# Expert weights in rows of 8 KB, and one pool of 8 KB places in place of pairs of 4 KB tiles

## The chip, the core and the metric

One core of one Trainium2 chip runs the whole program. The metric is the device time of one execution in microseconds. Before the change three runs took 1977.47, 1981.33 and 1982.41 us; their median is 1981.33 us.

## What is computed

Three blocks of a model run one after the other on 256 tokens of width 1024 in fp32. Only the end of the third block is touched here, the expert layer:

```python
def expert_choice_ffn(h, w_router, w_gate, w_up, w_down):
    b, s, d = h.shape
    cap = EC_CAPACITY * s // N_EXPERTS
    affinity = jax.nn.softmax((h @ w_router).astype(jnp.float32), axis=-1)
    top_val, top_idx = lax.top_k(affinity.transpose(0, 2, 1), cap)
    xe = jax.vmap(lambda hb, ib: hb[ib])(h, top_idx)
    act = jax.nn.silu(jnp.einsum('becd,edf->becf', xe, w_gate)) * jnp.einsum('becd,edf->becf', xe, w_up)
    ye = jnp.einsum('becf,efd->becd', act, w_down) * top_val[..., None].astype(h.dtype)
    return jax.vmap(lambda yb, ib: jnp.zeros((s, d), yb.dtype).at[ib.reshape(-1)].add(yb.reshape(-1, d)))(ye, top_idx)
```

There are 16 experts; each takes 32 of the tokens. An expert has a gate and an up matrix of 1024 x 2048 and a down matrix of 2048 x 1024, that is 8 MB each (here and below 1 MB of weights is 1024 KB, one load; GB/s count bytes in powers of ten). All 48 matrices, 384 MB, are read once from the chip's memory. After the experts comes the last norm.

## The kernel before, in words

`block3` ends with a product in split precision (`gemm_fm` with `tail=True`, called in `last`): `load_w` (L282) brings a chunk of weights into pool `ring`, and `split_w` (L287) splits it into a high and a low part, tiles `wh` and `wl` of pool `hl`. Its result, with the residual added (L1758), is the tile `x3a` of pool `res`. `experts` reads `x3a` for the router's logits (L1798), for the squares of the norm (L1790) and for the transposes that bring tokens into rows (L1824). Then follow the routing on VectorE, the one-hot matrices, and the gathers `pxe` (L1866) that build `xe`, the tokens of each expert.

The weights of the experts come through one function, `load` (L1876), always on SyncE's DMA queue, in program order. It goes round 21 places, each for 1 MB: 13 in the pools `er0` to `er3` on the right side of the memory, which open as earlier stages end, 3 in `ring`, 3 in `hl` and 2 in `res`. A place is free again when the matmuls on its last content are done. Places of `hl` are pairs of tiles of 128 x 1024, so that a load there is two DMAs of 512 KB (L1890, or L1892 in the last expert); all others are one tile of 128 x 2 x 1024 and one DMA (L1885), but for the last expert's down matrix, where there are two everywhere (L1892).

What one row of a DMA is differs. A piece of a gate or up matrix (`up`, L1902 its matmuls) is 128 rows of the matrix, and a row has 2048 numbers: 8 KB in one run, cut into two runs of 4 KB where the place is a pair. A piece of a down matrix is 256 rows of 1024 numbers, two runs of 4 KB in each partition (matmuls L1974). The last expert's down matrix is cut by columns, 512, 256 and 256 wide, so that the end of the kernel can begin on the first columns (matmuls L1996); its runs are 2 KB and then 1 KB.

The first expert's gate and up products (`pgu0`) use loads 1 to 16 and are made inside `experts`, between the gathers. `run` does the rest: loads 17 to 21, the first of the down matrix, go to `hl` and `res`, and load 22 takes the first place of `er0` again, when the first matmuls of `pgu0` are done. `body` opens the pool `ew` for `run` after block 3's pool has closed, and closes `hl` and `res` (`K.late`) after `run`.

Of the kernel before, what the change touches and what calls it, by code (L numbers as in the profile page):

```python
# [10 lines left out]
F32 = mybir.dt.float32  # L11
# [5 lines left out]

S = 256
D = 1024
BIG = 1e30  # L20
EPS = 1e-6

# [141 lines left out]
def layout(x):  # L164
    x = {k: np.asarray(v) for k, v in x.items()}
    a = {}
    ca, coff = const_pack()
    a.update(ca)
    parts = vec_parts(x)
    voff, _ = offsets(parts)  # L170
    a["vecs"] = np.ascontiguousarray(np.concatenate([np.asarray(v, np.float32) for v in parts.values()], 1))
    xt = lambda t: np.ascontiguousarray(t.T.reshape(8, 128, S).transpose(1, 0, 2))
    a["x"] = xt(x["x"][0])
    a["mem"] = xt(x["mem_3"][0])
    a["w_ada"] = np.ascontiguousarray(x["w_ada"][0].T.reshape(12, 2, 128, D).transpose(0, 2, 1, 3)).reshape(12, 128, 2 * D)
    a["crow"] = x["c"]
    w = x["w_in"][0]
    a["w_in"] = wchunks(np.concatenate([w[:, :2048], w[:, 2056:]], 1), 256)
    a["w_ba"] = np.ascontiguousarray(w[:, 2048:2056].reshape(8, 128, 8).transpose(1, 0, 2))
    rows = lambda *names: wchunks(np.concatenate([x[k][0] for k in names], 0), 256)  # L180
    a["w_mg1"] = rows("w_proj_dn", "w_proj_mb")
    a["w_out"] = wchunks(x["w_out"][0], 256)
    w = x["w_in_2"][0]
    a["w_in2"] = wchunks(np.concatenate([w[:, :1536], w[:, 1544:]], 1), 256)
    a["w_if"] = np.ascontiguousarray(w[:, 1536:1544].reshape(8, 128, 8).transpose(1, 0, 2))
    a["lru_w"] = np.ascontiguousarray(np.stack([
        x["lru_wa_2"][0].reshape(2, 128, 64), x["lru_wx_2"][0].reshape(2, 128, 64)], 0).transpose(2, 0, 1, 3))
    a["w_mg2"] = rows("w_out_lru_2", "w_out_mlstm_2", "w_out_sb_2")
    a["w_o2"] = wchunks(x["w_o_2"][0], 256)
    w = x["w_ffn_in_2"][0]  # L190
    a["w_f1"] = np.ascontiguousarray(np.concatenate(
        [w[:, :2816].reshape(1024, 22, 1, 128), w[:, 2816:].reshape(1024, 22, 1, 128)], 2).reshape(1024, 5632))
    a["w_f1"] = wchunks(a["w_f1"], 256)
    w = x["w_ffn_out_2"][0]
    a["w_f2a"] = wchunks(w[:1024], 256)
    a["w_f2b"] = wchunks(w[1024:2048], 256)
    a["w_f2c"] = wchunks(w[2048:], 256)
    a["w_in3"] = wchunks(x["w_in_3"][0], 256)
    pad = np.zeros((6, 7, 127), x["na_rpb_3"].dtype)
    pad[:, :, 48:79] = x["na_rpb_3"][0, :, 4:11]  # L200
    a["rpb"] = np.stack([pad[:, :, 63 - c:127 - c] for c in range(64)], 0)
    a["lora"] = np.ascontiguousarray(np.concatenate([x["rw_w2_3"][0], x["rw_a2_3"][0]], 1).transpose(1, 0, 2))
    a["g2"] = x["rw_g2_3"][0]
    a["w_mkv"] = wchunks(x["w_mem_kv_3"][0], 256)
    a["w_mg3a"] = rows("w_branch_na_3", "w_branch_mem_3")
    a["w_mg3b"] = rows("w_branch_rw_3")
    a["w_out3"] = wchunks(x["w_out_3"][0], 256)
    a["w_rt"] = np.zeros((128, 8, 32), x["w_router_3"].dtype)
    a["w_rt"][:, :, :16] = x["w_router_3"][0].reshape(8, 128, 16).transpose(1, 0, 2)
    a["w_eg"] = x["w_exp_gate_3"][0]  # L210
    a["w_eu"] = x["w_exp_up_3"][0]
    a["w_ed"] = x["w_exp_down_3"][0]
    a["g_fin"] = x["norm_final_g_3"].reshape(1, 1024)
    return {k: np.ascontiguousarray(v) for k, v in a.items()}, coff, voff

# [3 lines left out]
ES = [3, 3, 5, 2]  # L219
RB = 3  # L220
PB = [3, 3, 2]
HP = None
HB = 3


class Core:
# [1543 lines left out]
def experts(K, last, ep, tmp, pool, out):  # L1770

    nc, A, V, C, tc = K.nc, K.A, K.V, K.C, K.tc
# [43 lines left out]
    for t in range(2):  # L1816
        i = nc.scalar.activation(aff[:, t], zl[:, t], AF.Exp, scale=rs[:, t:t + 1], accum_out=su[:, t:t + 1])
# [52 lines left out]
        else:  # L1870
            nc.vector.tensor_scalar(d, p, V("g_ffn3", k), None, op0=ALU.mult)

    slots = [p for p, n in zip(K.er, ES) for _ in range(n)] + [K.ring] * RB + [K.hl] * HB + [K.res] * 2
    cnt = [0]

    def load(src, g=None):  # L1876

        pool = slots[cnt[0] % len(slots)]
        cnt[0] += 1
        if pool is K.hl:  # L1880
            w = [pool.tile([128, 1024], F32, tag=t, name="w" + t) for t in ("wh", "wl")]
        else:
            w = pool.tile([128, 2, 1024], F32, tag="x" if pool is K.res else "w", name="w")
            if g is None:
                nc.sync.dma_start(w, src.rearrange("i p n -> p i n"))  # L1885
                return w[:, 0], w[:, 1]
            w = w[:, 0], w[:, 1]
        for i in range(2):
            if g is None:
                nc.sync.dma_start(w[i], src[i])  # L1890
            else:
                nc.sync.dma_start(w[i].rearrange("p (g n) -> p g n", g=g), src[i].rearrange("g p n -> p g n"))  # L1892
        return w

    def up(src, e, before=None):
        pg = K.psum([128, 512], "pgu", "g")
        for k in range(8):
            if before is not None:
                before(k)
            w = load(src[e, k * 128:k * 128 + 128, :].rearrange("p (i n) -> i p n", i=2))  # L1900
            for j in range(4):
                nc.tensor.matmul(pg[32 * j:32 * j + 32], xe[:, k, e * 32:e * 32 + 32],  # L1902
                                 w[j // 2][:, j % 2 * 512:j % 2 * 512 + 512], start=k == 0, stop=k == 7)
        return pg
# [6 lines left out]
    def run(work):  # L1911
# [1 line left out]
        gr = work.tile([1, 1024], F32, name="gr")  # L1913
        sm = work.tile([128, 2, 3], F32, name="fsm")
        rs = work.tile([128, 2], F32, name="frs")
        parts = [(0, 512), (512, 768), (768, 1024)]

        def add(pvt, ye, c0, c1):

# [26 lines left out]
        for e in range(16):  # L1946
# [20 lines left out]
            pd = [K.psum([128, 512], f"pd{i}") for i in range(2)]  # L1967
            if e < 15:
                for c in range(8):
                    w = load(A["w_ed"][e, c * 256:c * 256 + 256, :].rearrange("(i p) n -> i p n", p=128))  # L1970
                    for i in range(2):
                        j, q = divmod(2 * c + i, 4)
                        for hh in range(2):
                            nc.tensor.matmul(pd[hh][32 * q:32 * q + 32], at[:, q, 32 * j:32 * j + 32],  # L1974
                                             w[i][:, hh * 512:hh * 512 + 512], start=j == 0, stop=j == 3)
                nc.scalar.copy(ye[:, 0:512], pd[0])  # L1976
                nc.vector.tensor_copy(ye[:, 512:1024], pd[1])  # L1977
                for c0 in (0, 512):
                    for _ in add(pvt, ye, c0, c0 + 512):
                        pass  # L1980
                continue
# [6 lines left out]
            for n, (c0, c1) in enumerate(parts):  # L1988
                m = c1 - c0
                g = 1024 // m  # L1990
                p = pd[c0 // 512][:, c0 % 512:c0 % 512 + m]
                for i in range(0, 16, 2 * g):
                    w = load(A["w_ed"][e, i * 128:(i + 2 * g) * 128, c0:c1].rearrange("(i g p) n -> i g p n", i=2, g=g), g)
                    for u in range(2 * g):
                        j, q = divmod(i + u, 4)
                        nc.tensor.matmul(p[32 * q:32 * q + 32], at[:, q, 32 * j:32 * j + 32],  # L1996
                                         w[u // g][:, u % g * m:u % g * m + m], start=j == 0, stop=j == 3)
                h = c0 + m // 2
                nc.scalar.copy(ye[:, c0:h], p[:, 0:m // 2])
                nc.vector.tensor_copy(ye[:, h:c1], p[:, m // 2:])  # L2000
                for t, a in add(pvt, ye, c0, c1):
                    finish(t, n, a)
# [6 lines left out]
@with_exitstack  # L2009
def body(ctx: ExitStack, tc: tile.TileContext, A, out, coff, voff):  # L2010
    nc = tc.nc
    K = Core(ctx, tc, A, coff, voff)
    K.load_vecs()
    K.load_consts("g", K.const)
    xt = K.res.tile([128, 8, S], F32, tag="x", name="x0")
    nc.sync.dma_start(xt, A["x"])
    mem = Memory(K)
    norms = TwoNorms(K)
    with tc.tile_pool(name="b1", bufs=1) as pool:
        xt = block1(K, xt, pool)  # L2020
    K.groups.pop("b1")
    with tc.tile_pool(name="b2", bufs=1) as pool:
        xt = block2(K, xt, pool, mem, norms)
    K.groups.pop("b2")
    with tc.tile_pool(name="b3", bufs=1) as pool:
        last = block3(K, xt, pool, mem, norms)
        ep = ctx.enter_context(tc.tile_pool(name="ep", bufs=1, side="right"))
        with tc.tile_pool(name="et", bufs=1) as tmp:
            run = experts(K, last, ep, tmp, pool, out)
    with tc.tile_pool(name="ew", bufs=1) as work:  # L2030
        run(work)
    K.late.close()

# [14 lines left out]
```

## Time and profile before

| | us |
|---|---|
| median of the runs | 1981.33 |
| the profiled execution's own time | 1979.57 |
| its span from first to last instruction | 1977.6 |
| TensorE busy | 1649.7 (83%) |
| VectorE busy | 771.7 (39%) |
| ScalarE busy | 590.2 (30%) |
| 16 DMA engines, mean rate over the span | 282 GB/s |

Busy times are those of one profiled execution. A TensorE matmul's end is modelled, so its busy share says little of how near to its peak it is. The mean rate hides two halves: up to about 1040 us the DMA engines are idle much of the time, and from there to the end they move the experts' weights.

### The profile page before, as it was taken

To read this page: it belongs to the slowest core of one execution; us is meant where nothing else is said; L and a number is where in the kernel's file an instruction comes from. 1 tells how busy PE (TensorE), PEld (TensorE's weight loads), DVE (VectorE), ACT (ScalarE), POOL (GpSimd) and SP (SyncE) were. 2 spreads that over 40 slices of the span, in tenths; PEclk is the share of its full clock that TensorE was granted. 3 is DMA by queue.
4 is the path that set the end of the run, shared out by engine and by line. 5 is a ranking of instruction groups with operands and counts; after the bars stand their busy time and mean duration, and the time that the engine had idled before them with its cause. 6 is when DMAs were issued, how large, how long until landed. Compare 5 with 4: busy or idle time off the path is not lost.

```text
span 1977.6 us, 28659 instructions
## 1 busy us (share of the span) xinstructions
PE 1649.7 (83%) x11882; PEld 1062.5 (54%) x11882; DVE 771.7 (39%) x1529; ACT 590.2 (30%) x1159; POOL 106.8 (5%) x123
## 2 busy tenths in 40 slices
PE   3999989999999999989979776677777677767776
PEld 2998989899999998868974111111111111111111
DVE  7797767657655676855571000000000000000001
ACT  3655555764554454633441000000000000000001
POOL 0000000000000121300020000000000000000000
PEclk9998989999999999979999888888878889777888
DMA  7442643344545553322689999999999999999998
GB/s 298 171 149 89 230 170 117 138 141 173 177 174 186 179 198 128 108 76 88 235 310 375 414 415 415 415 417 416 416 416 415 416 416 414 414 415 417 418 416 293
DMA packets 106917, 557.04 MB, mean 282 GB/s; under 512 B 10530, under 2 KB 17058, under 8 KB 61859
## 3 DMA queue, kind: packets, MB, share of 16 engines
q1 hardware_dynamic: 106786, 555.21, 72.1%
q8 instruction: 93, 1.52, 0.3%
q14 instruction: 38, 0.30, 0.0%
HBM read 554.12 MB, written 1.05 MB: 281 GB/s over the span
## 4 chain that ended last, share of the span: by engine, by line
PE 46%; DMA 41%; DVE 8%; ACT 2%; issue 1%; SPq 1%; POOL 1%; DVEq 0%; ACTq 0%
DMA w<-in_w_eg 15%; DMA w<-in_w_eu 13%; PE psg L313 10%; PE psg L311 10%; PE psg L312 10%; DMA w<-in_w_ed 5%; DMA wwl<-in_w_eu 4%; DVE wl L302 2%; PE pgu L1902 2%; PE pd L1974 2%; DMA wwh<-in_w_eu 1%; DVE w L664 1%; DMA wwl<-in_w_eg 1%; DMA wwh<-in_w_eg 1%; PE psg L328 1%
## 5 line engine op out<-in xcount | busy, mean ns | idle before, releaser
L1902 PE MATMUL pgu<-w,xe 128*32 128x512 f32 x1768 | 304.2, 782 | 155.1 <-DMA w<-in_w_eu 89.1
L302 DVE TENSOR_TENSOR wl<-w,wh 128x512 fp32r<-128x512 f32 (+1 forms) x510 | 330.6, 690 | 183.2 <-ACT wh L300 170.6
L300 ACT CAST wh<-w 128x512 fp32r<-128x512 f32 x516 | 287.7, 607 | 253.1 <-PE psg L312 223.3
L1902 PEld LDWEIGHTS pgu<-w,xe 128*32 128x32 f32 x1768 | 42.9, 121 | 393.6 <-DMA w<-in_w_eu 222.3
L1974 PE MATMUL pd<-w,at 128*32 128x512 f32 x808 | 186.0, 637 | 48.5 <-DMA w<-in_w_ed 43.0
L1952 DVE TENSOR_TENSOR gg<-gg,pgu 128x512 f32<-128x512 f32 x16 | 11.0, 688 | 503.9 <-PE pgu L1902 500.3
L1974 PEld LDWEIGHTS pd<-w,at 128*32 128x32 f32 x808 | 42.2, 115 | 183.5 <-DMA w<-in_w_ed 112.7
L1977 DVE COPY ye<-pd 128x512 f32<-128x512 f32 x15 | 10.4, 692 | 294.5 <-PE pd L1974 294.5
L313 PE MATMUL psg<-n3hh,wl 128*128 128x256 f32 x344 | 103.0, 299 | 3.2 <-POOL wl L302 1.7
L311 PE MATMUL psg<-h1h,wh 128*128 128x256 f32 x352 | 103.0, 293 | 0.0
L311 PE MATMUL psg<-n3hh,wh 128*128 128x256 f32 x344 | 101.5, 295 | 1.6 <-ACT wh L300 1.6
L313 PE MATMUL psg<-h1h,wl 128*128 128x256 f32 x352 | 102.2, 290 | 0.0
L312 PE MATMUL psg<-h1l,wh 128*128 128x256 f32 x352 | 101.7, 289 | 0.0
L1957 ACT COPY at<-pat 128x512 f32<-128x512 f32 x16 | 9.4, 585 | 308.6 <-PE pat L1955 297.1
L312 PE MATMUL psg<-n3hl,wh 128*128 128x256 f32 x344 | 100.8, 293 | 0.1
L312 PE MATMUL psg<-n2fhl,wh 128*128 128x256 f32 x352 | 100.0, 284 | 0.2
L313 PE MATMUL psg<-n2fhh,wl 128*128 128x256 f32 x352 | 99.8, 283 | 0.0
L311 PE MATMUL psg<-n2fhh,wh 128*128 128x256 f32 x352 | 99.6, 283 | 0.0
L1951 ACT ACTIVATE gg<-pgu 128x512 f32<-128x512 f32 x16 | 9.6, 597 | 277.3 <-PE pgu L1902 277.2
L311 PE MATMUL psg<-n2hh,wh 128*128 128x256 f32 x304 | 87.1, 287 | 2.0 <-ACT n2hh L453 2.0
L312 PE MATMUL psg<-n2hl,wh 128*128 128x256 f32 x304 | 87.7, 289 | 0.2 <-DVE n2hl L456 0.2
L1976 ACT COPY ye<-pd 128x512 f32<-128x512 f32 x15 | 8.8, 585 | 264.6 <-issue 257.3
(725 smaller groups left out, 3473.8 us busy)
## 6 DMA issues: line engine op xcount, KB each, us to landing
w<-in_w_eg SPq DMA_DIRECT2D x112, 1024.0 KB, 18.5
w<-in_w_eu SPq DMA_DIRECT2D x109, 1024.0 KB, 19.9
w<-in_w_ed SPq DMA_DIRECT2D x101, 1024.0 KB, 18.8
w<-in_w_in SPq DMA_DIRECT2D x68, 1024.0 KB, 4.8
w<-in_w_f SPq DMA_DIRECT2D x22, 1024.0 KB, 4.8
w<-in_w_ada SPq DMA_DIRECT2D x12, 1024.0 KB, 5.3
wwh<-in_w_ed SPq DMA_DIRECT2D x19, 512.0 KB, 14.7
wwl<-in_w_ed SPq DMA_DIRECT2D x19, 512.0 KB, 15.2
```

The lines of the kernel that those rows point to most:

```text
L300: self.nc.scalar.copy(wh[:, a:b], w[:, k0 + a:k0 + b])
L302: e.tensor_tensor(wl[:, a:b], w[:, k0 + a:k0 + b], wh[:, a:b], op=ALU.subtract)
L311: nc.tensor.matmul(out, a, x[0], start=first, stop=False)
L312: nc.tensor.matmul(out, a, x[1], start=False, stop=False)
L313: nc.tensor.matmul(out, b, x[0], start=False, stop=last)
L328: nc.tensor.matmul(out, xl[:, k, ts], wh[:, c0:c1], start=False, stop=False)
L664: nc.vector.scalar_tensor_tensor(w[:, f], w[:, f], 1.0, sg, op0=ALU.mult, op1=ALU.mult, accum_out=out[:, j:j + 1])
L1902: nc.tensor.matmul(pg[32 * j:32 * j + 32], xe[:, k, e * 32:e * 32 + 32], w[j // 2][:, j % 2 * 512:j % 2 * 512 + 512], start=k == 0, stop=k ...
L1951: nc.scalar.activation(gg, pgu[0], AF.Silu)
L1952: nc.vector.tensor_tensor(gg, gg, pgu[1], op=ALU.mult)
L1974: nc.tensor.matmul(pd[hh][32 * q:32 * q + 32], at[:, q, 32 * j:32 * j + 32], w[i][:, hh * 512:hh * 512 + 512], start=j == 0, stop=j == 3)
L1977: nc.vector.tensor_copy(ye[:, 512:1024], pd[1])
```

## The change

The host lays the down matrices out anew: for experts 0 to 14 as 8 pieces of 128 x 2048, where a partition's two runs of 4 KB stand behind each other, and for the last expert (`w_edl`) as 8 pieces of 128 x 2048 as well, in which all that a partition needs of a piece of 512 or 256 columns is one run. `load` has one form left: one tile of 128 x 2048, one DMA. The three pairs of `hl` and the two tiles of `res` are no places any more; `hl` and `res` are closed ahead of `run`, and a new pool `lw` of five tiles of 8 KB a partition is opened, which is as much memory as the two held (24 KB and 16 KB a partition). The order of the loads and the matmuls, and the number of places, stay.

```diff
+LAST = [(0, 512), (512, 768), (768, 1024)]
...
-    a["w_ed"] = x["w_exp_down_3"][0]
+    w = x["w_exp_down_3"][0]
+    a["w_ed"] = w[:15].reshape(15, 8, 2, 128, 1024).transpose(0, 1, 3, 2, 4).reshape(15, 8, 128, 2048)
+    last = []
+    for c0, c1 in LAST:
+        g = 1024 // (c1 - c0)
+        last.append(w[15, :, c0:c1].reshape(8 // g, 2 * g, 128, c1 - c0).transpose(0, 2, 1, 3).reshape(8 // g, 128, 2048))
+    a["w_edl"] = np.concatenate(last, 0)
...
+LB = 5
...
-    slots = [p for p, n in zip(K.er, ES) for _ in range(n)] + [K.ring] * RB + [K.hl] * HB + [K.res] * 2
+    slots = [p for p, n in zip(K.er, ES) for _ in range(n)] + [K.ring] * RB + [None] * LB
     cnt = [0]
 
-    def load(src, g=None):
-
-        pool = slots[cnt[0] % len(slots)]
+    def load(src):
+
+        pool = slots[cnt[0] % len(slots)] or K.lw
         cnt[0] += 1
-        if pool is K.hl:
-            w = [pool.tile([128, 1024], F32, tag=t, name="w" + t) for t in ("wh", "wl")]
-        else:
-            w = pool.tile([128, 2, 1024], F32, tag="x" if pool is K.res else "w", name="w")
-            if g is None:
-                nc.sync.dma_start(w, src.rearrange("i p n -> p i n"))
-                return w[:, 0], w[:, 1]
-            w = w[:, 0], w[:, 1]
-        for i in range(2):
-            if g is None:
-                nc.sync.dma_start(w[i], src[i])
-            else:
-                nc.sync.dma_start(w[i].rearrange("p (g n) -> p g n", g=g), src[i].rearrange("g p n -> p g n"))
-        return w
+        w = pool.tile([128, 2048], F32, tag="w", name="w")
+        nc.sync.dma_start(w, src)
+        return w[:, 0:1024], w[:, 1024:2048]
...
-            w = load(src[e, k * 128:k * 128 + 128, :].rearrange("p (i n) -> i p n", i=2))
+            w = load(src[e, k * 128:k * 128 + 128, :])
...
-        parts = [(0, 512), (512, 768), (768, 1024)]
+        parts = LAST
+        edl = iter(range(8))
...
-                    w = load(A["w_ed"][e, c * 256:c * 256 + 256, :].rearrange("(i p) n -> i p n", p=128))
+                    w = load(A["w_ed"][e, c])
...
-                    w = load(A["w_ed"][e, i * 128:(i + 2 * g) * 128, c0:c1].rearrange("(i g p) n -> i g p n", i=2, g=g), g)
+                    w = load(A["w_edl"][next(edl)])
...
+    K.late.close()
+    K.lw = ctx.enter_context(tc.tile_pool(name="lw", bufs=LB))
     with tc.tile_pool(name="ew", bufs=1) as work:
         run(work)
-    K.late.close()
```

## Rows read from the trace of the kernel before

**Rows 1.** The page, its head and the GB/s that 40 slices of the span moved

```profile
span 1977.6 us, 28659 instructions
...
GB/s 298 171 149 89 230 170 117 138 141 173 177 174 186 179 198 128 108 76 88 235 310 375 414 415 415 415 417 416 416 416 415 416 416 414 414 415 417 418 416 293
```

**Rows 2.** The chain of waits from 900 us on: start us, us, what

```profile
1055.22 0.99 PE pgu L1902 x8
...
1059.53 0.66 PE pxe L1866 x4
...
1761.57 1.98 PE pgu L1902 x8
...
1862.45 19.89 DMA w<-in_w_eu
```

**Rows 3.** Windows: us, busy of each engine (instructions), granted clock, DMA share, GB/s

```profile
1042.50:1945.00 902.50, 667.28 (x3258) 147.75 (x3256) 65.38 (x97) 35.82 (x69) 18.87 (x32) 0.86 1.02 415
1945.00:1967.00 22.00, 16.81 (x114) 5.33 (x114) 4.14 (x9) 6.24 (x15) 3.91 (x4) 0.92 0.90 302
```

**Rows 4.** Windows in which the weights move in rows of 8 KB alone

```profile
1055.00:1082.00 27.00, 27.00 (x200) 10.24 (x203) 5.59 (x9) 4.74 (x8) 3.52 (x6) 1.00 1.01 418
...
1418.00:1452.00 34.00, 23.93 (x120) 4.21 (x116) 3.44 (x5) 1.18 (x2) 0.00 (x0) 0.78 1.01 420
1843.00:1876.00 33.00, 23.19 (x120) 4.13 (x116) 3.44 (x5) 1.18 (x2) 0.00 (x0) 0.79 1.01 420
```

**Rows 5.** A window in which whole loads of a down matrix move in rows of 4 KB

```profile
1155.00:1170.00 15.00, 11.89 (x56) 3.85 (x54) 0.69 (x1) 0.86 (x2) 1.18 (x2) 0.82 1.03 409
```

**Rows 6.** A window in which halves of 512 KB move in rows of 4 KB

```profile
1138.00:1143.00 5.00, 4.32 (x20) 0.74 (x20) 0.00 (x0) 0.00 (x0) 0.00 (x0) 0.80 1.03 410
```

**Rows 7.** DMA packets, one a row, in 1418 to 1452 us

```profile
DMA packets 1963, 14.27 MB, mean 420 GB/s; under 512 B 222, under 2 KB 222, under 8 KB 222
```

**Rows 8.** DMA packets in 1155 to 1170 us

```profile
DMA packets 1594, 6.14 MB, mean 409 GB/s; under 512 B 95, under 2 KB 95, under 8 KB 1594
```

**Rows 9.** DMA packets and issues (count, KB each, us to landing) in 1042 to 1967 us

```profile
DMA packets 77573, 381.17 MB, mean 412 GB/s; under 512 B 6753, under 2 KB 10849, under 8 KB 51298
...
w<-in_w_eu SPq DMA_DIRECT2D x101, 1024.0 KB, 19.9
...
wwl<-in_w_eu SPq DMA_DIRECT2D x19, 512.0 KB, 15.0
```

**Rows 10.** Timeline of TensorE at the last expert: start us, us, engine, line, operation

```profile
1944.42 1.05 PE L1902 MATMUL pgu<-wwl,xe 128*32 128x512 f32 x4 [0.24 <-DMA wwl<-in_w_eu]
...
1953.88 1.05 PE L1996 MATMUL pd<-w,at 128*32 128x512 f32 x4 [0.28 <-DMA w<-in_w_ed]
...
1955.16 1.05 PE L1996 MATMUL pd<-w,at 128*32 128x512 f32 x4 [0.24 <-DMA w<-in_w_ed]
...
1966.95 0.64 PE L1996 MATMUL pd<-w,at 128*32 128x256 f32 x8 [0.79 <-DMA w<-in_w_ed]
```

**Rows 11.** Timeline of SyncE's queue, three places: start us, us, line, load

```profile
952.16 1.60 SPq L1885 DMA_DIRECT2D w<-in_w_eg  x3
...
1017.99 0.33 SPq L1890 DMA_DIRECT2D wwh<-in_w_ed  x1
...
1027.92 17.09 SPq L1885 DMA_DIRECT2D w<-in_w_ed  x4
```

**Rows 12.** SyncE's waits, 1024 to 1042 us: for whom, us in total, times, longest

```profile
SPq L1885 <- PE pgu L1902: 13.1, 1, 13.1
SPq L1885 <- PE ptm L1824: 2.5, 1, 2.5
```

**Rows 13.** Instructions on tile x3a: ns min/median/max, first and last start us

```profile
L1824 PE MATMUL ptm<-ct_g,x3a x16: 271/272/331, 1025.4 to 1027.6; 128*128 128x128 f32 x16
```

**Rows 14.** Windows around the gap in the DMA work, columns as in rows 3

```profile
1035.00:1037.50 2.50, 0.36 (x2) 0.29 (x2) 1.95 (x3) 0.00 (x0) 1.28 (x1) 0.50 0.23 90
...
1042.50:1045.00 2.50, 2.50 (x26) 1.30 (x24) 0.48 (x1) 0.47 (x1) 0.00 (x0) 1.00 0.96 283
```

## The prediction

> **What bounds the kernel now.** I read the page first, for where the time lies. The GB/s of its 40 slices [rows 1] fall into two parts: up to the 21st slice the rate swings between 76 and 310, from the 23rd to the 39th it stands at 414 to 418 and hardly moves. A rate that does not move while experts begin and end is that of something full. The chain of waits says the same: from about 1061 us on its long pieces are loads of some 20 us such as the one at 1862.45, with matmuls of 1 to 2 us between them [rows 2]. Then windows over this stretch: in 902.5 us TensorE is busy 667 us, 74%, while the 16 DMA engines show a share of 1.02 [rows 3]; more than 1 comes from packets that overlap, so they never pause. The end is therefore set by bytes over rate from about 1042.5 us to the last load's landing at 1966.9, and what is worth knowing is whether rate depends on the form of the loads.
>
> It does. I looked for windows in which one form alone moves. Rows of 8 KB (whole loads of gate and up matrices) move at 420 GB/s, in one window at 418 [rows 4]. Whole loads of a down matrix move at 409 [rows 5], and halves of 512 KB at 410 [rows 6]. The packets show that the form is what I take it for: in 1418 to 1452 us, 1963 - 222 = 1741 packets of 8 KB or more and none between 2 and 8 KB [rows 7], in 1155 to 1170 us almost none but 4 KB ones [rows 8]. The halves separate the causes: they hold parts of the same gate and up matrices that move at 420 as whole loads, and they are slower by as much as the down matrices; and being two DMAs for 1 MB costs nothing on top.
>
> **The change, part by part.** How much moves in 4 KB rows? Between 1042 and 1967 us there are 51298 packets under 8 KB, of which 10849 are under 2 KB [rows 9]. Of the 40449 between, the last expert's first 4 MB are 2048 rows of 2 KB by the code, which leaves 38401 rows of 4 KB: 150 MB. The other 205 MB before the last down matrix have rows of 8 KB already; there the change does nothing.
>
> 1. *Rows of 4 KB become rows of 8 KB.* 1 MB is 1.0486 million bytes: at 409.5 GB/s it takes 2.561 us, at 420 2.497, a gain of 0.064 us. For 150 MB: **-9.6 us**. The bounds come from the same rows: with 410 against 418 it is 0.049 us and -7.3, with 408.5 against 420.5 (the ends of rounding) 0.073 and -11.0. I take the middle, since two of three 8 KB windows give 420, and the one at 418 lies where places only begin to come free. New rows should be as good as those of the gate matrices, since they also read 1 MB in one run.
>
> Here the Trainium skill has a price too: "DMA: Bandwidth & Descriptors", section "Why small descriptors are slow", gives each packet a fixed overhead of about 3 cycles on top of one for each 32 bytes. That is 131/128 against 259/256, 1.2%, where the windows show 2.6%; by the page the step would be an estimated -4.3 us.
>
> 2. *The last expert's down matrix.* It now moves in rows of 2 and 1 KB. Its 8 MB take from the last up matrix's landing, 1944.4, to 1966.95, 22.5 us; at 8 KB rows 8 x 2.497 = 20.0: **-2.5 us**. Less than 1 us is not likely, since its two halves at 1953.88 and 1955.16 lie 1.28 us apart, as close as 4 KB halves do; 8 such halves make 10.2 of the 22.5 us, and the loss lies in the 1 KB part [rows 10]. At most it is 6: in the last 22 us only 6.64 million bytes move (302 GB/s, share 0.90 [rows 3]), which 420 would do in 15.8 us.
>
> 3. *One DMA where there were two.* After the last landing 8 matmul records of 0.64 us together used the last half [rows 10]; with 1 MB as one DMA all 16 come behind it: **+0.6 us**. Elsewhere matmuls that wait for the whole load end later by about 1 us, and that lies beside the next loads: a load lands 19.9 us after its issue at 2.5 us each, so eight are on their way [rows 9]. Fewer issues on SyncE's queue: 0, for the same reason.
>
> 4. *Five places that come free together.* Now the first of loads 17 to 21 goes out at 1018, as the single tiles of `hl` and then `res` come free, and the last at 1027.9 [rows 11], after a wait of 2.5 us for the transposes [rows 12]. A new pool over old memory can wait for all of the old pools; the pool `er` places at 952 came three at once [rows 11]. The last reader of `hl` and `res` is those transposes of `x3a`, which end at 1027.9 [rows 13]. So SyncE's queue would wait there, and behind it stand only load 22 and the next. Is that covered? Today the DMA work of these loads ends in the window from 1035 and starts again at about 1042.6 [rows 14]: all 21 places are full, and SyncE waits 13.1 us, to 1041.4, for the first matmuls of `pgu0` [rows 12]. From that issue to data are 1.2 us, so five loads from 1027.9 on move from 1029.1 to 1029.1 + 5 x 2.5 = 1041.6, and load 22 follows. The cover is just enough: **0 us**. If the release comes at a later time t, the price is t - 1029 us, one for one.
>
> Matmuls, their order and count, and all work ahead of 1018 us stay: 0. A load's 8 matmul records take 0.99 us at the full clock and 1.98 at half [rows 2], both below the 2.497 us of a load.
>
> Sum: -9.6 - 2.5 + 0.6 = -11.5 us. Span 1977.6 [rows 1] becomes 1966.1; the profiled execution's own time is 1979.57, which becomes 1968.1; the median of the runs is 1.76 above it, so the forecast is **1969.8 us**, 0.6% less. Both ends together: the small gains give -7.3 - 1.0 + 0.6 = -7.7 (1973.6), the large -11.0 - 6.2 + 0.6 = -16.6 (1964.7). For the runs' own scatter I set 1963.5 to 1975 for this case.
>
> **The rivals.** A run-to-run difference under 0.3%, 5.9 us, can't be told from no change here.
>
> *A. The five places come late (slower).* If the new pool's start is tied to block 3's whole pool, its last use is the gather that ends at 1060.2 [rows 2]. SyncE's queue is in order, so nothing is loaded from about 1020 until then. The full stretch would start at 1061.4 with 16 MB on the chip rather than at 1042.6 with 21: 18.8 + 12.5 = 31.3 us more, against -11.5: 2001 us. It costs from 1029 on, undoes the gain at 1040.5 and is slower by 0.3% from about 1046.4. For it speaks that `hl` and `res` are closed behind block 3's pool in the code, and that the price is one for one; against it that the new pool takes exactly their 40 KB and no byte of block 3's. Chance 0.06 for a slower time, 0.03 for one in which it eats only the gain.
>
> *B. Only part of the gap is the row's.* If some of the 2.6% between the forms went with what is beside them (which places, which stage), steps 1 and 2 would give half: -6.0 + 0.6 = -5.4, 1975.9, within 0.3%. Against it: a gate matrix shows both rates. The skill's 3 cycles (same page and section) come out here, an estimated -4.9 us with the last expert's rows; no row of this trace supports so small a difference. Chance 0.06.
>
> *C. TensorE takes over.* 74% busy over the stretch [rows 3], and SyncE does wait for matmuls at times. If its pace held the loads, only step 2 would be left: about 1979, within 0.3%. Against it: the 1.98 us at the slow clock. Chance 0.04.
>
> *D. The change does not do what it says*: rows of the new layout are cut into 4 KB again. Against it: the gate loads, with the same rows, are not. Then step 2 alone and about 1979. Chance 0.01.
>
> **How the numbers follow.** Forecast 0.80. Faster by over 0.3%: 0.80, with 0.02 from B's better half, 0.82. Within 0.3%: what is left of B, with C, D and A's small form, 0.12. Slower: A, 0.06. The range of 1963.5 to 1977 holds the forecast's own and B's.
>
> **What would show it.** Right: no packets between 2 and 8 KB after 1042 us; a rate of 420 in all slices from the 23rd to the 39th; the last down matrix's landings 2.5 us apart; five loads in a row on SyncE's queue at about 1028; DMA work at 1042 without a gap over 1 us. Step 1 is wrong if the mean rate stays under 418 with 8 KB rows alone; step 4 if the DMA engines are idle after 1030 us and the full stretch starts later than 1043.5; C is right if the DMA share falls under 1 while SyncE waits for matmuls.

## The result, and the profile after

The changed kernel takes 1966.88 us (median of 4 runs, 1962.31 to 1968.36), the kernel before 1979.82 us in 4 runs; the ratio is 0.9936, with a 95% interval of 0.9923 to 0.9949. That is 12.9 us or 0.64% less; 0.6% less was forecast, and the range held the time.

The profiled execution has a span of 1960.4 us, 17.2 less. Not all of that is the change's. These are its instructions on `x3a`, where the part that the change touches begins:

```profile
L1832 PE MATMUL ptm<-ct_g,x3a x16: 270/272/332, 1020.4 to 1022.6; 128*128 128x128 f32 x16
```

The transposes end at 1022.9, 5.0 us earlier than before [rows 13], after work that is the same in both kernels. Most of that comes up in one stretch, here as windows of the kernel before and of the changed one (us, busy time of each engine with instructions, granted clock, DMA share, GB/s; the granted clock is TensorE's, as a share of its full speed):

```profile
140.00:215.00 75.00, 71.74 (x772) 64.65 (x771) 57.43 (x150) 41.88 (x98) 0.78 (x2) 0.91 0.33 118
```

```profile
140.00:215.00 75.00, 71.36 (x806) 64.39 (x805) 60.28 (x156) 44.25 (x106) 0.78 (x2) 0.98 0.38 132
```

The granted clock was 0.91 there and 0.98 here, and in the same 75 us TensorE got through 34 more matmul records, at 75/806 us each some 3 us of the 5. It comes and goes between executions: in the profiles of the ten kernels below, whose computation up to here is the same, the transposes end anywhere from 1021.7 to 1030.5 us, and the profiled execution was the fastest of the four. I therefore count from the end of the transposes.

The page's GB/s of 40 slices and, below, a window and the DMA packets of the stretch in which the weights move:

```profile
GB/s 301 167 156 102 222 169 125 134 140 180 175 175 186 178 192 140 108 77 90 211 271 412 421 419 422 420 420 420 421 420 420 421 419 421 420 420 420 420 420 309
```

```profile
1042.50:1929.00 886.50, 642.35 (x3216) 137.13 (x3212) 64.34 (x95) 34.87 (x67) 18.88 (x32) 0.83 1.01 420
```

```profile
DMA packets 52086, 379.46 MB, mean 417 GB/s; under 512 B 5793, under 2 KB 5793, under 8 KB 5794
```

From the 23rd slice to the 39th the rate is 419 to 422 where it was 414 to 418 [rows 1]; the mean is 420 where it was 415 [rows 3]; of 4 KB packets, 38401 before [rows 9], none is left (the one between 512 B and 8 KB is the load of the last norm's gains). The timeline of TensorE at the last expert, its last up load and its last down load:

```profile
1928.80 1.84 PE L1899 MATMUL pgu<-w,xe 128*32 128x512 f32 x8 [0.54 <-DMA w<-in_w_eu]
...
1948.74 1.07 PE L1994 MATMUL pd<-w,at 128*32 128x256 f32 x16 [1.10 <-DMA w<-in_w_edl]
```

From the transposes' end to the last up load used, 1944.42 - 1027.9 = 916.5 us before [rows 10] are now 905.9: -10.6. From there to the last down load's use, 22.5 us are now 19.9: -2.6. From that to the end of the span, 10.7 us are now 11.7: +1.0. Together -12.2; the -5.0 from ahead of the transposes, which lies within that scatter, makes it 17.2.

### The profile page after: what moved, and what is told of

It is laid out like the page before. It is cut to its first block, busy times and chain, and to the rows that moved or that the text cites. A ratio compares the mean times of both kernels' runs of the same rounds, so it can differ in the third digit from the quotient of the medians.

```text
span 1960.4 us, 28542 instructions
## 1 busy us (share of the span) xinstructions
PE 1623.6 (83%) x11882; PEld 1047.8 (53%) x11882; DVE 771.7 (39%) x1529; ACT 590.2 (30%) x1159; POOL 105.5 (5%) x123
## 3 DMA queue, kind: packets, MB, share of 16 engines
HBM read 554.12 MB, written 1.05 MB: 283 GB/s over the span
## 4 chain that ended last, share of the span: by engine, by line
DMA 47%; PE 42%; DVE 8%; ACT 1%; issue 1%; POOL 1%; SPq 0%; DVEq 0%; ACTq 0%
DMA w<-in_w_eu 15%; DMA w<-in_w_eg 15%; DMA w<-in_w_ed 14%; PE psg L321 10%; PE psg L319 10%; PE psg L320 10%; DVE wl L310 2%; DMA w<-in_w_edl 1%; DVE w L672 1%; PE psg L335 1%; PE psg L336 1%; PE atps L489 1%; PE psg L337 1%; PE pgu L1899 1%; DMA w<-in_w_ada 0%
## 5 line engine op out<-in xcount | busy, mean ns | idle before, releaser
L1899 PE MATMUL pgu<-w,xe 128*32 128x512 f32 x2048 | 363.4, 806 | 167.9 <-DMA w<-in_w_eu 98.9
L1899 PEld LDWEIGHTS pgu<-w,xe 128*32 128x32 f32 x2048 | 50.4, 123 | 458.4 <-DMA w<-in_w_eu 262.5
L1972 PE MATMUL pd<-w,at 128*32 128x512 f32 x960 | 209.4, 624 | 52.4 <-DMA w<-in_w_ed 46.2
L1972 PEld LDWEIGHTS pd<-w,at 128*32 128x32 f32 x960 | 48.8, 113 | 204.4 <-DMA w<-in_w_ed 122.9
L321 PE MATMUL psg<-n2hh,wl 128*128 128x256 f32 x304 | 86.5, 285 | 0.0
## 6 DMA issues: line engine op xcount, KB each, us to landing
w<-in_w_eg SPq DMA_DIRECT2D x128, 1024.0 KB, 19.9
w<-in_w_eu SPq DMA_DIRECT2D x128, 1024.0 KB, 19.9
w<-in_w_ed SPq DMA_DIRECT2D x120, 1024.0 KB, 19.9
```

The source lines that it names most:

```text
L321: nc.tensor.matmul(out, b, x[0], start=False, stop=last)
```

## The experiments

Each is compared with the kernel before, which ran beside it on the same chip; between experiments I compare the ratios, since the kernel before had medians of 1974.9 to 1979.8 us in the different groups.

**New rows, old places.** The new layout of the down matrices, with the pairs in `hl` and the tiles in `res` as they were; a pair takes its load as two halves in 4 KB rows. The edit, against the changed kernel:

```diff
...
+        if pool is K.hl:
+            w = [pool.tile([128, 1024], F32, tag=t, name="w" + t) for t in ("wh", "wl")]
+            for i in range(2):
+                nc.sync.dma_start(w[i], src[:, i * 1024:i * 1024 + 1024])
+            return w
+        w = pool.tile([128, 2, 1024], F32, tag="x" if pool is K.res else "w", name="w")
+        nc.sync.dma_start(w.rearrange("p i n -> p (i n)"), src)
...
```

> The new layout of the down matrices with the old 21 places: loads in the pairs of hl still move as two halves in rows of 4 KB. Of the 150 MB in 4 KB rows, 51 go through those pairs after the first round (18 rounds of 3, less the first 3), so 99 MB gain 0.064 us each. Theory (the price is per row): -6.3 -2.5 for the last matrix +0.6 for its coarser end = -8.2 us against the kernel before, 1971.6 us at its median of 1979.8; 420 GB/s wherever no pair moves. Rival (the pairs and their doubled DMAs were the price): only the last matrix gains, -2 us, about 1978.

Measured: 1970.59 us, ratio 0.9967 (0.9946 to 0.9988), that is -6.5 us with an interval of -10.7 to -2.4. **New places, old rows**, the other half, against the kernel before:

```diff
...
+        w = pool.tile([128, 2, 1024], F32, tag="w", name="w")
+        if g is None:
+            nc.sync.dma_start(w, src.rearrange("i p n -> p i n"))
+        else:
+            for i in range(2):
+                nc.sync.dma_start(w[:, i].rearrange("p (g n) -> p g n", g=g), src[i].rearrange("g p n -> p g n"))
...
```

> The new pool of five places with the old layout: gate and up loads are rows of 8 KB everywhere (35 MB change), down loads stay at 4 KB, the last matrix at 2 and 1 KB. Theory: -2.2 us, 1977.6 us; the five loads go out together after the transposes and cost nothing, so that the full stretch begins as long after the transposes as before. Rival (the late release costs): the full stretch begins up to 6 us later and the kernel is no faster or slower than before, 1980 to 1984. Rival (pairs were the price): -10 us, 1970.

Measured: 1977.14 us, ratio 0.999 (0.9975 to 1.0005), -2.0 us, an interval that holds no change. The times alone would leave the split loose; the windows from 1100 to 1900 us are sharper. First the kernel before, then new rows alone, new places alone, and both:

```profile
1100.00:1900.00 800.00, 581.11 (x2708) 122.07 (x2708) 53.72 (x78) 26.54 (x52) 14.17 (x24) 0.85 1.02 415
```

```profile
1100.00:1900.00 800.00, 584.53 (x2730) 123.24 (x2731) 54.81 (x80) 27.13 (x53) 14.17 (x24) 0.85 1.02 419
```

```profile
1100.00:1900.00 800.00, 570.70 (x2719) 117.29 (x2718) 53.68 (x78) 26.55 (x52) 14.17 (x24) 0.82 1.02 416
```

```profile
1100.00:1900.00 800.00, 572.15 (x2750) 116.75 (x2750) 57.11 (x83) 27.13 (x53) 14.17 (x24) 0.83 1.01 420
```

If nothing but the share of 4 KB rows counts, with 2.561 and 2.497 us for 1 MB, 150 of 355 MB in such rows give a mean of 415.4 GB/s, the 51 left to the pairs 418.4, and the 115 of the down matrices (15 x 8 less the 5 loaded ahead) 416.5. The windows say 415, 419 and 416. The pairs' doubled DMAs show no price besides their rows. The place change opens the last 16 MB only together with the row change, since a down load in a pair needs both.

**Late places.** 1 KB of padding pushes the new pool so far that its end lies on block 3's memory.

```diff
+    pad = ctx.enter_context(tc.tile_pool(name="pad", bufs=1)).tile([128, 256], F32, name="pad")
+    nc.gpsimd.memset(pad[:, 0:1], 0.0)
     K.lw = ctx.enter_context(tc.tile_pool(name="lw", bufs=LB))
```

> The changed kernel with 1 KB of padding in front of the new pool, so that its last place lies over 1 KB of block 3's memory. Theory: the whole pool then waits for block 3's pool, whose last use is the last gather, some 32 us after the transposes; loads from the 17th on wait behind it on the in-order queue, and the kernel takes 31 us more than the changed one, about 1998 us. Rival (only the tile that overlaps waits): 4 places come as before and the price is under 3 us. Rival (work beside it covers the wait): under 10 us.

Measured: 1981.41 us, ratio 1.0022 (1.0011 to 1.0034). Against the changed kernel's 0.9936 that is 0.86%, 17 us: the change's gain and more is lost, but only about half of the price that I gave. SyncE's queue shows why; then its wait for the gathers, where the last gather ends (instructions of its line) and the DMA windows:

```profile
1038.51 3.54 SPq L1889 DMA_DIRECT2D w<-in_w_ed  x3
1042.59 5.50 SPq L1889 DMA_DIRECT2D w<-in_w_eg  x4
1060.69 2.51 SPq L1889 DMA_DIRECT2D w<-in_w_ed  x5
```

```profile
SPq L1889 <- PE pxe L1874: 12.5, 1, 12.5
```

```profile
L1874 PE MATMUL pxe<-oh,hth x32: 277/280/553, 1034.6 to 1060.2; 128*128 128x256 f32 x32
```

```profile
1020.00:1035.00 15.00, 5.91 (x56) 4.54 (x56) 11.21 (x28) 6.91 (x13) 5.04 (x3) 0.77 0.00 1
1057.00:1062.00 5.00, 5.00 (x43) 2.01 (x45) 0.49 (x1) 1.80 (x3) 1.22 (x3) 1.00 0.32 97
```

All five loads wait for the last use of block 3's pool, as the theory says, though by the layout only the last place lies over that pool: they go out at 1060.69, behind the gather's end at 1060.2 + 0.3. But they do not block the queue. Seven loads that the program's text has behind them, for places that come free by the first products of `pgu0`, stand ahead of them: the order on the queue is not that of the text. What sets it, no run here shows. So the DMA engines lose the five loads' 12.5 us and a pause of 0.68 x 5 = 3.4 us, 15.9 of the 17, rather than 31.

**Waits tile by tile.** The new pool takes over old memory place by place.

```diff
-    K.lw = ctx.enter_context(tc.tile_pool(name="lw", bufs=LB))
+    K.lw = ctx.enter_context(tc.tile_pool(name="lw", bufs=LB, reuse_waits="tile"))
```

> The changed kernel with the new pool waiting tile by tile for the memory it takes over rather than for both old pools as a whole. Theory: loads 17 to 20 go out 4 to 10 us earlier, the DMA engines pause after them instead of before them, and the time is that of the changed kernel, 1966.9 us, within 1 us. Rival (the cover of the five late loads was not enough): up to 3 us less.

Measured: 1963.12 us, ratio 0.993 (0.9913 to 0.9948), not to be told from the changed kernel's 0.9936. The loads go out from 1016.1 on, and the pause moves behind them:

```profile
1016.13 22.63 SPq L1889 DMA_DIRECT2D w<-in_w_ed  x8
```

```profile
1025.00:1030.00 5.00, 0.00 (x0) 0.00 (x0) 4.79 (x9) 2.37 (x3) 4.60 (x2) 0.50 1.01 423
1030.00:1035.00 5.00, 3.86 (x22) 2.48 (x26) 2.29 (x6) 0.47 (x1) 0.12 (x1) 0.52 0.17 70
```

The times can't tell the theory from the rival of up to 3 us less. Counted from the transposes' end, the profiled execution leaves 1958.2 - 1021.7 = 936.5 us here and 1960.4 - 1022.9 = 937.5 in the changed kernel, so the five late loads cost about 1 us at most, by one profile of each.

**Only the row length.** Two kernels keep the changed one's places, order and one DMA for each load, and cut each partition's 8 KB into 2 runs of 4 KB or 4 of 2 KB.

```diff
+    cut = lambda t: t.reshape(t.shape[:-1] + (2, 1024)).swapaxes(-2, -3)
...
-        nc.sync.dma_start(w, src)
+        nc.sync.dma_start(w.rearrange("p (i n) -> p i n", n=1024), src.rearrange("i p n -> p i n"))
```

> The changed kernel, its pool and its order of loads, with every load of expert weights cut into rows of 4 KB (two runs for each partition, one DMA). Theory (a fixed price for each row, 8 ns by the two rates of before): 363 MB x 0.064 us = +23 us on the changed kernel's 1966.9, 1990 us, at 409 to 410 GB/s. Rival (half of the gap is something else): +12, 1978.5. Beside it, the Trainium skill (DMA: Bandwidth & Descriptors, Why small descriptors are slow) with 3 cycles for each packet would give an estimated 1.2% of 906 us, +10.

Measured: 1989.43 us, ratio 1.0055 (1.004 to 1.007); 1.19% or 23.5 us above the changed kernel's ratio.

> The same with rows of 2 KB (four runs for each partition). Theory: with 8 ns for each row 1 MB takes 2.497 + 24 x 0.008 = 2.689 us, 390 GB/s; 363 MB x 0.192 = +70 us, 2037 us. Rival (half of the gap is something else): +35, 2002. Rival (short rows are cheap down to some size, or SyncE's queue becomes the bound with 512 rows a load): under +25, or over +100.

Measured: 2044.12 us, ratio 1.033 (1.0304 to 1.0357); 3.94% or 78 us above. Windows of the two, 4 KB first:

```profile
1100.00:1900.00 800.00, 557.17 (x2676) 112.93 (x2674) 53.73 (x78) 26.57 (x52) 14.17 (x24) 0.82 1.03 409
```

```profile
1100.00:1900.00 800.00, 576.92 (x2534) 112.46 (x2526) 50.27 (x73) 25.38 (x50) 15.35 (x26) 0.72 1.05 387
```

1 MB takes 2.710 us at 387 GB/s, 2.564 at 409 and 2.497 at 420. From 2 to 4 KB each of the 16 engines has 16 rows fewer for 0.146 us, 9.1 ns a row; from 4 to 8 KB 8 fewer for 0.067 us, 8.4 ns (an estimate, with the rows spread evenly over the engines). By the MB that moved in these 800 us (309.27, 327.34 and 336.23), which are finer than whole GB/s, it is 9.4 and 8.5 ns. That is nearly one price for a row, a little above the 8 ns that the kernel before gave. How far apart the rows start in memory shows no effect: 4 KB in the first of these kernels, 8 KB for the halves of the kernel before [rows 6], and they move at 409 and 410. Where in the transfer the price arises, no run shows. The Trainium skill's 3 cycles ("DMA: Bandwidth & Descriptors", section "Why small descriptors are slow") lie in the same direction and are too small: an estimated +10 us for 4 KB rows, where +23.5 was measured.

**Longer rows.** If a row has a price, 8 KB need not be the end. I made the places of a pool regions of one tile, with all the weights in one stream of 1 MB units that the host lays out in the order of use, first as a control with the same rows:

```diff
+            r, at, u, n = next(loads)
...
+                    homes[r] = pool.tile([128, sum(GROUPS[r]) * 2048], F32, tag="w", name=f"wx{r}")
+                w = homes[r][:, at * 2048:(at + n) * 2048]
+            nc.sync.dma_start(w, A[f"w_x{n}"][c])
```

> A control for the next kernel: the same rows of 8 KB, the same 21 places and order, but the places of a pool are regions of one tile and the loads come from one host-made stream of 1 MB units. All theories: the changed kernel's 1966.9 us within 2 us.

Measured: 1965.39 us, ratio 0.993 (0.9903 to 0.9958), as expected. Then `GROUPS` fills several neighbouring places by one DMA: twos first.

> From the second round on, 14 of each 21 places are filled in pairs by one DMA of 2 MB in rows of 16 KB; the other 7, the first round and the last 8 MB stay at 1 MB and 8 KB. Theory (a fixed price for each row): 1 MB in 16 KB rows takes 2.465 us, 425 GB/s; about 236 MB x 0.0325 = -7.7 us on the changed kernel, 1959 us. Rival (8 KB rows are at the limit of the engines): no gain, 1967 us, 420 GB/s. Rival (pairs come free too late and the engines starve): slower than 1970.

Measured: 1955.46 us, ratio 0.9881 (0.9858 to 0.9904), -10.9 us against the changed kernel's ratio, where -7.7 was expected; an interval of some 4.5 us to either side holds both.

> The stream of the kernel with rows of 16 KB, with longer rows from the second round on: of each 21 places 12 are filled by threes (3 MB, rows of 24 KB), 6 by twos (16 KB), the three of ring one by one. Theory (a fixed price for each row; 16 KB rows were measured at 0.046 us for each MB below 8 KB rows, so 24 KB ones should be at 0.046 x 4/3 = 0.061): (12 x 0.061 + 6 x 0.046) / 21 x 355 MB = -17 us on the changed kernel's 1966, 1949 us. Rival (longer than 16 KB gains nothing): 18 places at 0.046, -14, 1952. Rival (a load of 3 MB waits for three places, the engines starve): the DMA share falls under 1 and the kernel is no better than the one with 16 KB rows, 1955 or more.

Measured: 1955.49 us, ratio 0.9887 (0.9861 to 0.9912), the same as twos: -9.7 us against the changed kernel's ratio, where -17 was expected.

> The same with the two pools of five places filled at once (5 MB, rows of 40 KB), two pools of three by threes, one by two, ring one by one. Theory: 40 KB rows at 0.046 x 8/5 = 0.074: (10 x 0.074 + 6 x 0.061 + 2 x 0.046) / 21 x 355 = -20 us, 1946 us. Rival (starving): 5 MB can only be asked for when all five places are used up, a quarter of all the memory; the DMA share falls under 1 and the time is above that of the kernel with 24 KB rows.

Measured: 1949.81 us, ratio 0.9864 (0.9841 to 0.9886). It has the lowest median of all, 14 us below the changed kernel by the ratios, where 20 were expected. The intervals of twos, threes and fives overlap; counted from the transposes' end, the profiles leave 929.3, 929.2 and 922.3 us, and 937.5 in the changed kernel. Windows in the middle, 16 KB rows and then, as the DMA packets of that stretch, threes and fives:

```profile
1100.00:1900.00 800.00, 522.56 (x2780) 129.05 (x2780) 57.69 (x84) 28.02 (x55) 15.35 (x26) 0.80 1.01 425
```

```profile
DMA packets 22255, 342.10 MB, mean 428 GB/s; under 512 B 2473, under 2 KB 2473, under 8 KB 2474
```

```profile
DMA packets 17910, 343.09 MB, mean 429 GB/s; under 512 B 1987, under 2 KB 1987, under 8 KB 1988
```

There the rates are close to what the price of a row asks for: with the 2.452 us of 1 MB in 16 KB rows (from 425 for a mix of two thirds such rows and one third at 2.497), 24 and 40 KB rows and their mixes work out at 428 and 430 GB/s. By the MB moved in the 800 us (342.10 and 343.09, against 336.23 with 8 KB rows) the 355 MB take 15 and 18 us less, of the 17 and 20 expected. Most of the rest was lost at the two ends of the stretch. First 30 us that begin 5 us after the transposes' end, in the changed kernel, with twos, with threes and with fives:

```profile
1027.90:1057.90 30.00, 25.58 (x183) 11.75 (x183) 8.86 (x16) 4.03 (x8) 3.00 (x2) 0.86 0.99 406
```

```profile
1035.10:1065.10 30.00, 25.50 (x172) 11.69 (x173) 8.45 (x15) 4.11 (x8) 3.08 (x2) 0.81 0.93 381
```

```profile
1029.70:1059.70 30.00, 25.57 (x174) 11.75 (x174) 8.38 (x15) 4.05 (x8) 3.02 (x2) 0.83 0.84 350
```

```profile
1030.50:1060.50 30.00, 25.49 (x183) 11.69 (x183) 8.94 (x16) 4.12 (x8) 3.09 (x2) 0.86 0.91 381
```

A load of two or more places waits until all of them are used up, and while the first expert's products use the places up one by one, the engines pause: a share of 0.84 instead of 0.99 for 30 us is 4.5 us with threes, 0.91 is 2.4 with fives. Then the end, TensorE and a DMA window with threes, and TensorE with fives:

```profile
1920.34 4.86 PE L1929 MATMUL pgu<-wx,xe 128*32 128x512 f32 x24 [6.27 <-DMA wx<-in_w_x]
...
1942.40 1.93 PE L2023 MATMUL pd<-wx,at 128*32 128x256 f32 x32
```

```profile
1938.00:1944.00 6.00, 5.29 (x70) 2.55 (x68) 2.99 (x7) 2.65 (x9) 3.32 (x4) 1.00 0.03 10
```

```profile
1937.23 1.07 PE L2023 MATMUL pd<-wx,at 128*32 128x256 f32 x16 [1.39 <-DMA wx<-in_w_x]
```

With threes the last up load is one of 3 MB; with fives, by the code, the last 14 MB come singly, since a group that no longer fits is taken apart. With threes TensorE waits 6.27 us for that load and then has the products of all three places to make at once, 24 records; from there on it is TensorE that runs late. The DMA engines are done soon after 1938, and the last products begin only at 1942.40, some 4 us behind the last landing, where with fives they begin as it lands. The 3 us of the rates, the 2 of the start and these 4 are more than enough for the 6.9 us (929.2 - 922.3) between threes and fives; how they share it stays open, since no run changes the groups at one end alone. Single loads in the second round and at the last expert would be the next thing to try.

## Why the prediction was right

*What bounds.* Bytes over rate, as forecast: the DMA share of the stretch is 1.02 before and 1.01 after, and the times of the other kernels follow their rates but for the ends of the stretch.

*Step 1, the rows: -9.6.* Measured -10.6 us to the last up load, and 420 GB/s throughout. That the price belongs to the row, and not to the pairs, the stage or the places, is shown by the two halves of the change and by the kernel in which nothing but the row length differs (+23.5 us measured, 23 worked out from the windows of before). The term is 1 us small, and more than half of that lies in the price: the prediction took 0.064 us for 1 MB from whole GB/s in short windows, and the kernels with 4 and with 8 KB rows alone give 0.068 by their MB, -10.2 us for 150 MB. Rivals B and D fall with it; the DMA packets show no row cut.

*Step 2, the last matrix: -2.5.* Measured -2.6. *Step 3, one DMA for two: +0.6.* The 16 matmul records behind the last landing take 1.07 us where 8 took 0.64; the stretch behind it grew by 1.0 us in all. The rest lies in the four matmul records of the products after it, 1.75 us where they took 1.13, in a window in which the granted clock was 0.61, a mean between its two levels, against 1.00 before; why it was lower there no run shows. The kernel before, then the changed one:

```profile
1968.00:1971.00 3.00, 1.13 (x4) 0.68 (x4) 1.41 (x5) 1.41 (x7) 0.00 (x0) 1.00 0.00 0
```

```profile
1950.00:1954.00 4.00, 1.75 (x4) 0.92 (x4) 1.36 (x5) 1.79 (x9) 0.00 (x0) 0.61 0.00 0
```

*Step 4, the places: 0.* They came free together right behind the transposes, and the queue's next loads followed almost without a pause. SyncE's queue, its waits between 1018 and 1040 us, and the windows in which the five loads end and the next ones begin:

```profile
1022.92 17.12 SPq L1889 DMA_DIRECT2D w<-in_w_ed  x8
```

```profile
SPq L1889 <- PE pgu L1899: 12.0, 2, 11.0
SPq L1889 <- PE ptm L1832: 9.0, 1, 9.0
```

```profile
1035.00:1037.50 2.50, 2.50 (x18) 0.60 (x11) 0.00 (x0) 0.31 (x1) 0.00 (x0) 0.78 0.90 341
1037.50:1040.00 2.50, 2.50 (x26) 1.37 (x25) 0.49 (x1) 0.47 (x1) 0.00 (x0) 1.00 0.84 305
```

Shares of 0.90 and 0.84 are 0.65 us of pause. The wait for the transposes grew from 2.5 us [rows 12] to 9.0 and cost about 1 us at most, as the variant that waits tile by tile shows. Rival A described a real mechanism, which 1 KB of padding brings about, but its price was wrong, 17 us and not 31: the step "SyncE's queue is in order, so nothing is loaded until then" took the order of the program's text for the order on the queue. *Rival C*: with 40 KB rows the weights come at 429 GB/s, and from 1100 to 1900 us TensorE still keeps up (DMA share 1.00).

## What to carry to other kernels

Where a stretch moves bytes at a rate that nothing changes, look for windows in which one form of load moves alone; if two forms differ in rate, the gain is the megabytes of the slower form times the difference, and it arrives in full as long as the engines never pause. Make rows as long as the layout lets you, beyond 8 KB too, but let a longer load not wait for more places than come free together: at the start of a stretch short loads fill better, and at its end the last long load brings its products all at once. A place that comes free late costs little as long as its loads still move before the next places come free; what its delay would cost is read from the order in which the queue was really built.

## What was not expected of the hardware

The price of a row hardly depends on its length: by the MB moved from 1100 to 1900 us, it is 9.4 ns from 2 to 4 KB, 8.5 from 4 to 8, and about 10 from 8 to 16 KB (339.98 MB with two thirds in 16 KB rows: 0.041 us for 4 rows fewer on each engine). So rows of 8 KB, which looked like the end of it at a DMA share of 1.01, were not: a share of 1 in the windows says that the engines never paused, not that they moved what they could: shares of 1.00 to 1.05 went with 387 to 429 GB/s.
